# Feed-forward layers in three pieces of 8, 7 and 7 tile pairs, with weight slots of 1024 columns

## The chip, the cores and the metric

The kernel runs on one core of a Trainium2 chip, as one launch that holds the whole network. The metric is the device time of one execution in microseconds (us); three executions of the kernel before are given with their median. A profiled execution of the same kernel supplies the trace that is quoted here. In it PE is TensorE (matmuls), PEld its weight loads, DVE is VectorE, ACT ScalarE, POOL GpSimd, SP SyncE (it only issues DMAs here).

## The reference: what is computed

Two layers act on 256 latent tokens (stream 0) and 256 context tokens (stream 1), width 1024. Each layer is a half-step feed-forward, a token mixer (layer 0: neighbourhood attention beside a Hyena operator; layer 1: retention), and another half-step feed-forward. Every step is modulated: vectors of shift, scale and gate come from one large matrix applied to a conditioning vector.

```python
def modulate(x, gain, shift, scale):
    return rms_norm(x, gain) * (1 + scale) + shift

def swiglu(h, w_in, w_out):
    a, b = jnp.split(h @ w_in, 2, axis=-1)
    return (jax.nn.silu(a) * b) @ w_out
...
x_lat = x_lat + 0.5 * mod_l[:, 2] * swiglu(modulate(x_lat, norm_gain[i, 0], mod_l[:, 0], mod_l[:, 1]),
                                           ffn_a_in[i], ffn_a_out[i])
```

`w_in` is 1024 by 5632, `w_out` 2816 by 1024, so the hidden width 2816 is 22 tiles of 128 for `a` and 22 for `b`: 22 pairs. There are four such layers here. Three treat both streams; the last treats the latent stream alone, since nothing reads the context after it.

## The kernel before: tiling, staging and order

Activations are kept with features on partitions: a tile is 128 features by 512 columns, stream 0 in columns 0 to 255 and stream 1 in 256 to 511. Every product is done in three matmuls (L208, L209, L210), because weights and activations are each split into a high and a low part: high by high, low activation by high weight, high activation by low weight.

**Weights** form one long list, `worder`, in the order in which they are used. `w_dma` (L138) loads the next tile of the list into a slot of pool `wraw` on SP's queue. `w_split` makes the high part on ACT (`whi`, L89) and the low part on DVE (`wlo`, L153) into pool `whl`, and then issues one more load. `w_get(ahead)` first splits up to `ahead` tiles beyond the wanted one. Before, both pools have four slots of 11 x 128 = 1408 columns. An input tile (`ffi`) has 1024 columns, an output tile (`ffo`) has 1408. `w_paged` splits a tile into pages of 512 columns instead (`wphi`, `wplo`), from a general pool.

**A feed-forward layer** (`ffn`) goes in two halves of 11 pairs. For each pair two input tiles of 24 matmuls each run (`pi`), then `evac` makes silu(a) x b: silu on ACT, the product on DVE (`sg`, L580), the high part on ACT (`ghi`, L89) and the low part on DVE (`glo`, L181). After 11 pairs `out_gemm` runs the output: for each of 8 output tiles m the 11 x 3 matmuls of the half (`po`), then one DVE instruction for each stream adds gate times the sum to the residual `x` (L391). Both halves add to the same `x`.

**The modulation vectors** of later steps are made beside all this, on DVE: `mod_step` takes one tile of the modulation matrix and runs one or two reductions of 1024 columns (L237, `junk`): two where both streams need the vector, one where only the latent stream does (the last 32 of the 128 tiles). Two steps follow each pair's `evac`, and one step each output tile of `out_gemm`, except from m = 4 on where a norm follows. The steps work off one list of 128 tiles and stop when it is empty.

**The end of the last half** is special, because the next step's norm must be hidden. With `norm` given, every `x` is also squared on ACT and added up in `acc` on DVE (L269). The last `ntail` output tiles run stream 0 first, for all of them; then part of stream 1 of the first of them; then a matmul of ones (`ss`, L296) sums `acc` of stream 0; then the rest of stream 1. While that runs, ACT and DVE compute the inverse root (L283 to L287) and the first normed blocks (`nh` L308, `hhi` on ACT, `hlo` L313). `first_group` then begins the next step's matmuls (`fg`): two blocks of stream 0, then the matmul `ss` of stream 1, and so on. `ntail` is 3 where the output has 8 tiles of depth (the first mixer), and 2 where it has 11 (the feed-forward layers).

Nothing reorders the instructions: each engine runs its own in the order in which the Python code issues them, and waits in place.

Of the kernel before, what the change touches and what calls it, by code (L numbers as in the profile page):

```python
# [16 lines left out]
P = 128  # L17
D = 1024
KB = D // P
# [1 line left out]
TOK = 2 * L  # L21
DFF = 2816
NJ = DFF // P
NH = NJ // 2
EPS = 1e-6
MAGIC = 12582912.0
TWO_PI = float(np.nextafter(np.float32(2 * math.pi), np.float32(0)))
LOG_SET = "natural_log_exp_and_others"
WSLOT = NH * P


C_GAIN = 0
# [22 lines left out]
def body(ctx, tc, I, out):  # L55
    nc = tc.nc
    V, S, T, SY, G = nc.vector, nc.scalar, nc.tensor, nc.sync, nc.gpsimd

    wraw = ctx.enter_context(tc.tile_pool(name="wraw", bufs=4))
    whl = ctx.enter_context(tc.tile_pool(name="whl", bufs=4))  # L60
    modp = ctx.enter_context(tc.tile_pool(name="modp", bufs=2))
    one = ctx.enter_context(tc.tile_pool(name="one", bufs=1))
    pagep = ctx.enter_context(tc.tile_pool(name="pagep", bufs=1))
# [46 lines left out]
        worder.append((I[name][idx], n))  # L110

    def add_ffn(i):
        for h in range(2):
            for j in range(h * NH, (h + 1) * NH):
                add_w("ffi", (i, 2 * j), KB * P)
                add_w("ffi", (i, 2 * j + 1), KB * P)
            for m in range(KB):
                add_w("ffo", (i, h, m), NH * P)

    add_ffn(0)  # L120
    for b in range(24 + 8):
# [257 lines left out]
    def out_gemm(acts, nk, tiles_per_m, l, n, lat_only, norm, late_acts=None):  # L379
# [18 lines left out]
            for fn in late:  # L398
                fn()

        ntail = 3 if nk == KB else 2
        last_full = KB - ntail if (norm and not lat_only) else KB
        for m in range(last_full):
            if m == 0 and late_acts:
# [27 lines left out]
        if not norm:  # L432
            return
        ws = [w_get(3 - i) for i in range(ntail)]
        wfirst.extend(w_get(0) if i < 4 - ntail else w_paged() for i in range(3))
        pp = [ps(name="po") for _ in range(ntail)]
        for i in range(ntail):
            mm(pp[i], 0, L, [ws[i]], 0, L)
            run(evac(pp[i], 0, 0, last_full + i))
        cut = 5 if nk > KB else KB  # L440
        mm(pp[0], L, TOK, [ws[0]], L, TOK, 0, cut)
        norm.stream(0)
        mm(pp[0], L, TOK, [ws[0]], L, TOK, cut, nk)
# [22 lines left out]
    def first_group(norm, mid=None):  # L466

        w = list(wfirst)
        wfirst.clear()
        p = [ps(name="fg") for _ in range(4)]  # L470

        def mm(t, k, s):
            mm3k(p[t][:, s * L:(s + 1) * L], w[t], k, H[k], s * L, (s + 1) * L)

        for k in range(KB):
            for t in range(3):
                mm(t, k, 0)
            if k == 1:
                st = norm.steps(1)
                for kk in range(4, KB):  # L480
                    norm.blocks(0, (kk,))
                    next(st, None)
                norm.flush()
                norm.done(0)
                w.append(w_get(0))
                norm.blocks(1, range(KB))
                norm.flush()
                norm.done(1)
        for k in range(KB):
            mm(3, k, 0)  # L490
        w_split()
        for k in range(KB):
            for t in (0, 1):
                mm(t, k, 1)
        w_split()
        w_split()
        if mid:
            mid(p)
        for k in range(KB):
            for t in (2, 3):  # L500
                mm(t, k, 1)
        w_drop(w[2])
        return p

# [65 lines left out]

    def ffn(l, n, norm_in, norm_out, lat_only=False):
        w = L if lat_only else TOK
        for h in range(2):
            Gt = []

            def evac(pa, pb, shift=None):
                sg = page([P, w], name="sg")
# [13 lines left out]
            if h == 0:  # L591
# [14 lines left out]
                    p = first_group(norm_in, lambda p: evac(p[0], p[1]))  # L606
                    evac(p[2], p[3])
                j0 = len(Gt)
            for j in range(j0, NH):
                pa = in_tile(0, w)  # L610
                pb = in_tile(0, w)
                evac(pa, pb)
                if next(FILT["gen"], True):
                    mod_step(2)
            if h == 1:
                h_free()
            if h == 0:
                set_gate(l, n)
            pend_free.extend(Gt)
            out_gemm(Gt, NH, 1, l, n, lat_only, norm_out if h == 1 else None)  # L620
            free_acts()


# [828 lines left out]
def _layout(inp):  # L1452
# [49 lines left out]
    for l in range(2):  # L1502
        for nm in "ab":
            t_ = feat_tiles(g[f"ffn_{nm}_in"][l], 0)
            ffi.append(np.stack([t_[:NJ], t_[NJ:]], axis=1).reshape(2 * NJ, P, D))
            wo = g[f"ffn_{nm}_out"][l]
            ffo.append(np.stack([feat_tiles(wo[h * NH * P:(h + 1) * NH * P], 0) for h in range(2)]))
    z["ffi"] = np.stack(ffi)
    z["ffo"] = np.stack(ffo)

    def tok_tiles(w):
        C = w.shape[1]
# [64 lines left out]
```

## Time and profile before

| | |
|---|---|
| three runs | 1879.28, 1880.52, 1880.73 us; median 1880.52 us |
| profiled execution | 1878.3 us |
| its span, first to last instruction | 1876.5 us |
| mean granted TensorE clock in it | 0.997 |
| PE busy | 1857.1 us, 9974 matmuls |
| DVE busy | 1205.4 us |
| ACT busy | 701.5 us |
| POOL busy | 131.0 us |

The profiled execution took 1.8 us more than its span, and 2.2 us less than the median of the runs. A row of a timeline shows the start in us from the span's start, the duration, engine, line, operation, what it writes and reads, and how often it came in a row ("x2"); in brackets the idle time of the engine before it, and what ended it. A duration includes a tail that overlaps the next instruction, so the pace of a row of instructions is read from start to start. A row of a table of stretches shows the stretch, its length, the busy time of PE, PEld, DVE, ACT and POOL with the number of instructions, the granted clock, the DMA share and GB/s.

### The profile page before, as it was taken

The numbers are of one execution on the slowest core, as the hardware profiler recorded it, in microseconds if no ns is written. First come the engines' busy times: TensorE is split into PE (matmuls) and PEld (weight loads), VectorE is DVE, ScalarE is ACT, GpSimd is POOL, SyncE is SP. The second block draws the span as 40 slices with busy tenths as digits, with TensorE's granted clock in tenths as the row PEclk, the third lists the DMA queues.
The fourth block names the chain that finished last, engine by engine and source line by source line (L and its number), as shares of the span: only waits on it lengthen the run. The fifth ranks groups of instructions, "written<-read, shape, count | busy, mean of one in ns | idle before, by whom it ended". The sixth has DMA issues, their size and how long they took to land.

```text
span 1876.5 us, 25048 instructions
## 1 busy us (share of the span) xinstructions
PE 1857.1 (99%) x9974; PEld 1574.5 (84%) x9974; DVE 1205.4 (64%) x1858; ACT 701.5 (37%) x1085; POOL 131.0 (7%) x201
## 2 busy tenths in 40 slices
PE   8999999999999999999999999999999999999999
PEld 5788888898777898888888988888889888899999
DVE  5577677867687767866775655433456765567554
ACT  4332122335574342212233432122234454455342
POOL 2020000002003001100010001000000111000000
PEclk9999999999999999999999999999999999999999
DMA  9356445522323425644563356323323423355653
GB/s 361 127 176 218 144 169 206 197 79 80 101 70 100 145 69 185 217 160 158 195 231 112 108 189 220 101 90 108 106 85 97 140 90 101 104 183 187 190 186 130
DMA packets 77895, 277.45 MB, mean 148 GB/s; under 512 B 8657, under 2 KB 9681, under 8 KB 77650
## 3 DMA queue, kind: packets, MB, share of 16 engines
q1 hardware_dynamic: 58194, 206.64, 32.2%
q0 software_dynamic: 19584, 69.21, 11.7%
q8 instruction: 78, 1.28, 0.3%
q14 instruction: 39, 0.32, 0.1%
HBM read 274.77 MB, written 1.05 MB: 147 GB/s over the span
## 4 chain that ended last, share of the span: by engine, by line
PE 96%; DVE 2%; ACT 1%; issue 0%; DMA 0%; POOL 0%; DVEq 0%; ACTq 0%; POOLq 0%
PE pi L208 16%; PE pi L209 16%; PE pi L210 16%; PE po L210 9%; PE po L208 9%; PE po L209 9%; PE fg L208 2%; PE fg L210 2%; PE fg L209 2%; PE pv L1323 2%; PE pv L1324 2%; PE pv L1322 2%; PE pg L1324 1%; PE pg L1323 1%; PE pg L1322 1%
## 5 line engine op out<-in xcount | busy, mean ns | idle before, releaser
L208 PE MATMUL pi<-hhi,whi 128*128 128x512 f32 (+1 forms) x1488 | 544.2, 366 | 0.0
L209 PE MATMUL pi<-hlo,whi 128*128 128x512 f32 (+1 forms) x1488 | 543.9, 366 | 0.0
L210 PE MATMUL pi<-hhi,wlo 128*128 128x512 f32 (+1 forms) x1488 | 543.2, 365 | 0.0
L153 DVE TENSOR_TENSOR wlo<-raw,whi 128x1024 fp32r<-128x1024 f32 (+1 forms) x325 | 422.0, 1314 | 165.1 <-ACT whi L89 164.8
L89 ACT ACTIVATE whi<-raw 128x1024 fp32r<-128x1024 f32 (+1 forms) x329 | 364.4, 1116 | 418.8 <-issue 182.7
L208 PEld LDWEIGHTS pi<-hhi,whi 128*128 128x128 f32 x1488 | 279.3, 188 | 51.7 <-issue 1.5
L210 PEld LDWEIGHTS pi<-hhi,wlo 128*128 128x128 f32 x1488 | 279.3, 188 | 48.8
L209 PEld LDWEIGHTS pi<-hlo,whi 128*128 128x128 f32 x1488 | 279.4, 188 | 48.2
L237 DVE CUSTOM_DVE_ANT_0 junk<-wm,scb,cst 128x1024 bf16<-128x1024 f32 x224 | 287.3, 1283 | 14.1 <-DMA wm<-in_wmt_dram 9.0
L208 PE MATMUL po<-ghi,whi 128*128 128x512 f32 (+1 forms) x770 | 269.0, 349 | 0.0
L210 PE MATMUL po<-ghi,wlo 128*128 128x512 f32 (+1 forms) x770 | 268.4, 349 | 0.0
L209 PE MATMUL po<-glo,whi 128*128 128x512 f32 (+1 forms) x770 | 268.1, 348 | 0.0
L89 ACT ACTIVATE ghi<-sg 128x512 fp32r<-128x512 f32 (+1 forms) x88 | 50.9, 579 | 344.9 <-DVE sg L580 341.7
L209 PEld LDWEIGHTS po<-glo,whi 128*128 128x128 f32 x770 | 144.9, 188 | 20.4
L210 PEld LDWEIGHTS po<-ghi,wlo 128*128 128x128 f32 x770 | 144.9, 188 | 20.3
L208 PEld LDWEIGHTS po<-ghi,whi 128*128 128x128 f32 x770 | 144.8, 188 | 20.3
L391 DVE SCALAR_TENSOR_TENSOR x<-po,gate,x 128x256 f32<-128x256 f32 x136 | 61.4, 481 | 152.6 <-PE po L210 152.4
L580 DVE TENSOR_TENSOR sg<-sg,pi 128x512 f32<-128x512 f32 (+1 forms) x79 | 49.2, 622 | 138.1 <-PE pi L210 138.1
L222 POOL DMA_DIRECT2D wm<-in_wmt_dram x128 | 67.7, 529 | 785.5 <-DVE mod L237 766.2
L181 DVE TENSOR_TENSOR glo<-sg,ghi 128x512 fp32r<-128x512 f32 (+1 forms) x88 | 55.1, 626 | 56.9 <-ACT ghi L89 56.9
L89 ACT ACTIVATE sq<-x 128x256 f32<-128x256 f32 (+1 forms) x71 | 30.2, 439 | 132.5 <-DVE x L391 132.4
L208 PE MATMUL fg<-hhi,whi 128*128 128x256 f32 (+1 forms) x200 | 60.0, 300 | 0.0
(333 smaller groups left out, 2232.1 us busy)
## 6 DMA issues: line engine op xcount, KB each, us to landing
raw<-in_ffi_dram SPq DMA_DIRECT2D x176, 512.0 KB, 4.2
wm<-in_wmt_dram POOLq DMA_DIRECT2D x128, 512.0 KB, 3.8
raw<-in_ffo_dram SPq DMA_DIRECT2D x64, 704.0 KB, 5.4
raw<-in_rt_dram SPq DMA_DIRECT2D x64, 512.0 KB, 3.6
raw<-in_ev_dram SPq DMA_DIRECT2D x32, 512.0 KB, 3.6
wm<-in_wm_dram SPq DMA_DIRECT2D x32, 256.0 KB, 5.4
x<-in_xt_dram SPq DMA_DIRECT2D x8, 256.0 KB, 4.9
bias<-in_rpb_dram SPq DMA_DIRECT2D x8, 256.0 KB, 4.1
```

Source lines behind the costliest of these rows:

```text
L89: S.activation(out=out, in_=in_, func=func, **k)
L153: V.tensor_tensor(out=lo[:, :n], in0=t[:, :n], in1=f(hi[:, :n]), op=ALU.subtract)
L181: V.tensor_tensor(out=lo, in0=src, in1=f(hi), op=ALU.subtract)
L208: T.matmul(o, lhsT=w[0][:, c0:c1], rhs=x[0][:, x0:x1], start=start, stop=False)
L209: T.matmul(o, lhsT=w[0][:, c0:c1], rhs=x[1][:, x0:x1], start=False, stop=False)
L210: T.matmul(o, lhsT=w[1][:, c0:c1], rhs=x[0][:, x0:x1], start=False, stop=stop)
L222: G.dma_start(out=t, in_=I["wmt"][n])
L237: V.tensor_tensor_reduce(out=junk, in0=t, in1=scb[:, s, :], scale=1.0, scalar=bcol, op0=ALU.mult, op1=ALU.add, accum_out=MOD[l][:, idx, b, ...
L391: V.scalar_tensor_tensor(out=xs(s, m), in0=p[:, c0:c0 + L], scalar=gate[:, m, s:s + 1], in1=xs(s, m), op0=ALU.mult, op1=ALU.add)
L1322: T.matmul(po[tb], lhsT=H[k][0][:, hs_], rhs=w[0][:, ws_], start=k == 0, stop=False)
L1323: T.matmul(po[tb], lhsT=H[k][0][:, hs_], rhs=w[1][:, ws_], start=False, stop=False)
L1324: T.matmul(po[tb], lhsT=H[k][1][:, hs_], rhs=w[0][:, ws_], start=False, stop=k == KB - 1)
```

## The change

Each feed-forward layer goes in three pieces of 8, 7 and 7 pairs. All three add into `x`. The output weights are three arrays (`ffo0`, `ffo1`, `ffo2`) with 1024, 896 and 896 columns a tile; the arithmetic is the same, only grouped differently. The slot of both weight pools shrinks to 1024 columns, `wraw` gets six slots and `whl` five.

The conditions follow: `ntail` is 3 where the depth is at most 8, so now for the feed-forward layers too; of the first three weight tiles of the next step two come through `w_get` and one through `w_paged`, in the first mixer too (before, one and two there); and `cut`, the depth of stream 1 that the first tail tile runs ahead of the matmul `ss`, is at most the depth itself, 7, so all of that tile's stream 1 stands ahead of it (before, 5 of 11).

```diff
-NH = NJ // 2
+PIECES = ((0, 8), (8, 15), (15, 22))
-WSLOT = NH * P
+WSLOT = KB * P
...
-    wraw = ctx.enter_context(tc.tile_pool(name="wraw", bufs=4))
-    whl = ctx.enter_context(tc.tile_pool(name="whl", bufs=4))
+    wraw = ctx.enter_context(tc.tile_pool(name="wraw", bufs=6))
+    whl = ctx.enter_context(tc.tile_pool(name="whl", bufs=5))
...
     def add_ffn(i):
-        for h in range(2):
-            for j in range(h * NH, (h + 1) * NH):
+        for h, (j0, j1) in enumerate(PIECES):
+            for j in range(j0, j1):
                 add_w("ffi", (i, 2 * j), KB * P)
                 add_w("ffi", (i, 2 * j + 1), KB * P)
             for m in range(KB):
-                add_w("ffo", (i, h, m), NH * P)
+                add_w(f"ffo{h}", (i, m), (j1 - j0) * P)
...
-        ntail = 3 if nk == KB else 2
+        ntail = 3 if nk <= KB else 2
...
-        wfirst.extend(w_get(0) if i < 4 - ntail else w_paged() for i in range(3))
+        wfirst.extend(w_get(0) if i < 5 - ntail else w_paged() for i in range(3))
...
-        cut = 5 if nk > KB else KB
+        cut = min(5 if nk > KB else KB, nk)
...
+        w_drop(w[1])
         w_drop(w[2])
...
-        for h in range(2):
+        for h, (jf, jl) in enumerate(PIECES):
             Gt = []
+            last = h == len(PIECES) - 1
...
-            for j in range(j0, NH):
+            for j in range(jf + j0, jl):
...
-            if h == 1:
+            if last:
                 h_free()
...
-            out_gemm(Gt, NH, 1, l, n, lat_only, norm_out if h == 1 else None)
+            out_gemm(Gt, jl - jf, 1, l, n, lat_only, norm_out if last else None)
```

Where the instructions stand shows on DVE, at the end of the first feed-forward layer. First place: output tile m = 1 of its last piece, from the low part of the weights that is split ahead of it to the one after it. Before:

```order
L153 TENSOR_TENSOR wlo<-raw,whi 128x1408
L391 SCALAR_TENSOR_TENSOR x_94<-po,gate,x_94 128x256
L391 SCALAR_TENSOR_TENSOR x_102<-po,gate,x_102 128x256
L269 TENSOR_TENSOR acc<-acc,sq 128x256 x2
L237 ISA junk,mod_85<-wm,scb,cst 128x1024
L237 ISA mod_85 128x1
```

and now:

```order
L153 TENSOR_TENSOR wlo<-raw,whi 128x896
L391 SCALAR_TENSOR_TENSOR x_94<-po,gate,x_94 128x256
L391 SCALAR_TENSOR_TENSOR x_102<-po,gate,x_102 128x256
L269 TENSOR_TENSOR acc<-acc,sq 128x256 x2
L237 ISA junk,mod_85<-wm,scb,cst 128x1024
L237 ISA mod_85 128x1
```

The last two rows come twice for each such tile, in both. What a tile asks of DVE is the same but for the width of the weights, 896 columns and not 1408, while PE's share of the tile goes from 33 matmuls to 21.

Second place: the tail of the same layer, on DVE, from the last tile that runs both streams together to the last sum of stream 0. Before:

```order
L391 SCALAR_TENSOR_TENSOR x_106<-po,gate,x_106 128x256
L269 TENSOR_TENSOR acc<-acc,sq 128x256 x2
L153 TENSOR_TENSOR wlo<-raw,whi 128x1024
L181 TENSOR_TENSOR wplo<-raw,wphi 128x512 x2
L391 SCALAR_TENSOR_TENSOR x_100<-po,gate,x_100 128x256
L269 TENSOR_TENSOR acc<-acc,sq 128x256
L391 SCALAR_TENSOR_TENSOR x_100<-po,gate,x_100 128x256
L269 TENSOR_TENSOR acc<-acc,sq 128x256
```

and now:

```order
L391 SCALAR_TENSOR_TENSOR x_106<-po,gate,x_106 128x256
L269 TENSOR_TENSOR acc<-acc,sq 128x256 x2
L153 TENSOR_TENSOR wlo<-raw,whi 128x1024 x2
L181 TENSOR_TENSOR wplo<-raw,wphi 128x512 x2
L391 SCALAR_TENSOR_TENSOR x_98<-po,gate,x_98 128x256
L269 TENSOR_TENSOR acc<-acc,sq 128x256
L391 SCALAR_TENSOR_TENSOR x_100<-po,gate,x_100 128x256
L269 TENSOR_TENSOR acc<-acc,sq 128x256
L391 SCALAR_TENSOR_TENSOR x_100<-po,gate,x_100 128x256
L269 TENSOR_TENSOR acc<-acc,sq 128x256
```

One more low part of weights and one more residual tile of stream 0 stand ahead of the last sum.

Third place: DVE right behind the matmul `ss` of stream 0 in the same layer, up to the first normed block. Before:

```order
L287 SCALAR_TENSOR_TENSOR rr<-rs_m,rr 128x256
L308 SCALAR_TENSOR_TENSOR nh<-x_94,gs_88,rr 128x256
L391 SCALAR_TENSOR_TENSOR x_108<-po,gate,x_108 128x256
L308 SCALAR_TENSOR_TENSOR nh<-x_94,gs_88,rr 128x256
L313 SCALAR_TENSOR_TENSOR hlo<-nh,mod_85,hhi 128x256
```

and now:

```order
L287 SCALAR_TENSOR_TENSOR rr<-rs_m,rr 128x256
L391 SCALAR_TENSOR_TENSOR x_106<-po,gate,x_106 128x256
L269 TENSOR_TENSOR acc<-acc,sq 128x256
L308 SCALAR_TENSOR_TENSOR nh<-x_94,gs_88,rr 128x256
L391 SCALAR_TENSOR_TENSOR x_108<-po,gate,x_108 128x256
L308 SCALAR_TENSOR_TENSOR nh<-x_94,gs_88,rr 128x256
L313 SCALAR_TENSOR_TENSOR hlo<-nh,mod_85,hhi 128x256
```

A residual tile of stream 1 and its sum have moved ahead of the first normed block.

More of the change, by code (lines that the diff above doesn't have):

```diff
@@ L1506, in _layout @@
             wo = g[f"ffn_{nm}_out"][l]
-            ffo.append(np.stack([feat_tiles(wo[h * NH * P:(h + 1) * NH * P], 0) for h in range(2)]))
+            ffo.append([feat_tiles(wo[j0 * P:j1 * P], 0) for j0, j1 in PIECES])
     z["ffi"] = np.stack(ffi)
-    z["ffo"] = np.stack(ffo)
+    for h in range(len(PIECES)):
+        z[f"ffo{h}"] = np.stack([o[h] for o in ffo])
     def tok_tiles(w):
```

## The prediction

> **What bounds the kernel now.** I read the page's first part, then the chain that ended last, then the table of stretches, then PE's waits.
>
> ```profile
> PE 1857.1 (99%) x9974; PEld 1574.5 (84%) x9974; DVE 1205.4 (64%) x1858; ACT 701.5 (37%) x1085; POOL 131.0 (7%) x201
> PE 96%; DVE 2%; ACT 1%; issue 0%; DMA 0%; POOL 0%; DVEq 0%; ACTq 0%; POOLq 0%
> ```
>
> PE is busy for 1857.1 of 1876.5 us. All that any change of order or buffers could win is the rest, 19.4 us. The stretches show where that rest lies and how fast a PE that never waits goes:
>
> ```profile
> 0.00:50.00 50.00, 41.91 (x205) 27.32 (x206) 28.40 (x76) 21.38 (x41) 9.61 (x33) 0.97 1.01 362
> ...
> 400.00:500.00 100.00, 98.36 (x568) 84.62 (x567) 67.90 (x113) 53.37 (x96) 10.71 (x8) 1.00 0.25 81
> 500.00:600.00 100.00, 97.24 (x552) 76.17 (x551) 79.49 (x165) 57.39 (x157) 10.83 (x11) 0.98 0.28 93
> 600.00:700.00 100.00, 96.46 (x616) 87.12 (x616) 74.06 (x127) 43.36 (x73) 10.09 (x11) 0.98 0.31 103
> ...
> 1200.00:1300.00 100.00, 100.00 (x433) 80.94 (x432) 34.21 (x39) 25.08 (x31) 0.00 (x0) 1.00 0.28 89
> ...
> 1700.00:1800.00 100.00, 100.00 (x853) 100.00 (x852) 61.92 (x78) 48.54 (x70) 0.00 (x0) 1.00 0.61 190
> 1800.00:1877.00 77.00, 73.26 (x623) 73.06 (x622) 38.42 (x45) 28.23 (x36) 0.00 (x0) 0.99 0.47 151
> ```
>
> The row at 1200 lies inside a feed-forward layer: 433 matmuls of 512 columns touch these 100 us, so 432 steps of 0.2315 us, none lost. The row at 1700, with 256 columns, gives 0.117 us. In the first mixer (400 to 700) PE idles 1.6, 2.8 and 3.5 us, 7.9 in all; 8.1 lie in the first 50 us and 3.7 in the last 77. The feed-forward layers between have no idle time to win. The question is what the change makes PE wait for, and the answer must come from DVE, which each piece loads anew.
>
> **The change part by part. PE's own work** does not move. The matmuls of 512 and 256 columns are the same in number but for 6 halves that become 3 wholes in each of three tails (6 x 0.117 against 3 x 0.2315: nothing). A new output tile costs PE no gap, as the full rows above contain such switches. Eight more output tiles for each layer are eight more sets of residual updates on DVE, 0.79 us each (357.00 to 357.79, below), beside PE's 4.9 us for a tile.
>
> **Piece boundaries.** An output tile needs the last pair's `glo` at its last depth: now 22 matmuls (depth 8) or 19 (depth 7) after its start, not 31.
>
> ```profile
> 130.55 0.39 PE L208 MATMUL pi<-hhi,whi 128*128 128x512 f32 x1
> 132.38 0.69 DVE L181 TENSOR_TENSOR glo<-sg,ghi 128x512 fp32r<-128x512 f32 x1 [0.83 <-ACT ghi L89]
> ...
> 1841.80 0.28 PE L208 MATMUL po<-ghi,whi 128*128 128x256 f32 x1
> 1842.98 0.42 DVE L181 TENSOR_TENSOR glo<-sg,ghi 128x256 fp32r<-128x256 f32 x1 [0.48 <-ACT ghi L89]
> ```
>
> The first two rows are the end of pair 7 of the first layer, where piece 0 will end. DVE is late there, and still `glo` lands at 133.07, 2.5 us after PE goes on; PE would ask for it 22 x 0.2315 = 5.1 us after. The last two are the one-stream layer, the tightest: `glo` lands 1.6 us after the start, and 19 x 0.117 = 2.2 us are allowed. Cost 0; with DVE 3 us later than that it would be 0.5 us at a two-stream boundary and 2.4 at a one-stream one.
>
> **Buffers.** The loads and splits keep their order; deeper pools only let them run sooner. In the whole trace PE's waits name a weight split twice:
>
> ```profile
> PE fg L878 <- DVE wlo L170: 0.3, 1, 0.3
> PE po L210 <- DVE wlo L153: 0.2, 1, 0.2
> ```
>
> So a gain of at most 0.5 us here; I take 0 and leave what lies beyond to a rival.
>
> **The tails** are where I find the cost. From now on the feed-forward tails have the form of the first mixer's tail: `ntail` 3. So its rows price them.
>
> ```profile
> 646.41 0.28 PE L208 MATMUL po<-chi,whi 128*128 128x256 f32 x1
> ...
> 657.82 0.59 PE L296 MATMUL ss<-acc,cst 128*128 128x256 f32 x2
> ...
> 666.52 0.70 PE L296 MATMUL ss<-acc,cst 128*128 128x256 f32 x2 [0.28 <-DVE acc L269]
> ...
> 646.62 0.88 DVE L391 SCALAR_TENSOR_TENSOR x<-po,gate,x 128x256 f32<-128x256 f32 x2
> ...
> 656.13 0.43 DVE L269 TENSOR_TENSOR acc<-acc,sq 128x256 f32<-128x256 f32 x1 [0.48 <-ACT sq L89]
> ...
> 666.04 0.42 DVE L269 TENSOR_TENSOR acc<-acc,sq 128x256 f32<-128x256 f32 x1
> ```
>
> From the first `ss` (657.82) to the second (666.52) are 8.70 us, and the second waited for DVE's `acc`, which ended at 666.46: a chain on DVE sets this. Now the feed-forward tail before:
>
> ```profile
> 1026.63 0.64 PE L296 MATMUL ss<-acc,cst 128*128 128x256 f32 x2
> ...
> 1035.29 0.59 PE L296 MATMUL ss<-acc,cst 128*128 128x256 f32 x2
> ```
>
> 8.66 us, with no wait on the second: here PE sets it, with 51 + 18 = 69 half-width matmuls between the two. Now 42 + 18 = 60 stand there (two tails of 7 x 3, not 18 + 33), so PE needs 8.66 - 9 x 0.117 = 7.61, while DVE gets the mixer's list and needs 8.70. PE waits 1.1 us for each tail; the nine matmuls have gone ahead of `ss`, where they hide nothing that was open. **Three tails: 3.3 us.**
>
> Ahead of `ss`, the mixer's DVE chain takes 656.56 - 646.62 = 9.94 us from the residual of the last whole tile (m = 4) to the end of `acc`: one `wlo`, four `wplo` and three residual tiles with their sums. The changed list is one `wlo` of 1024 more for two `wplo` fewer:
>
> ```profile
> 396.15 1.22 DVE L153 TENSOR_TENSOR wlo<-raw,whi 128x1024 fp32r<-128x1024 f32 x1 [0.52 <-ACT whi L89]
> 397.30 1.29 DVE L181 TENSOR_TENSOR wplo<-raw,wphi 128x512 fp32r<-128x512 f32 x2
> 398.50 0.48 DVE L391 SCALAR_TENSOR_TENSOR x<-po,gate,x 128x256 f32<-128x256 f32 x1
> ```
>
> 1.15 against 1.20 us from start to start: the same. PE covered it in the mixer with 96 half matmuls, 657.82 - 646.41 = 11.41 us, and `ss` came 1.26 after `acc` was done. Now it has 7 x 3 x 4 = 84, which is 84 x 11.41 / 96 = 9.98 us. DVE needs 646.62 - 646.41 + 9.94 + 0.06 (from `acc` to `ss`, 666.46 to 666.52) = 10.21. So `ss` waits 0.2 us where DVE reaches m = 4 on time.
>
> In the first layer it does not. Its last piece begins with DVE behind, since the modulation steps of the last pair (four reductions) follow `glo`:
>
> ```profile
> 348.01 0.39 PE L208 MATMUL po<-ghi,whi 128*128 128x512 f32 x1
> ...
> 355.46 1.62 DVE L153 TENSOR_TENSOR wlo<-raw,whi 128x1408 fp32r<-128x1408 f32 x1
> 357.00 0.87 DVE L391 SCALAR_TENSOR_TENSOR x<-po,gate,x 128x256 f32<-128x256 f32 x2
> 357.79 1.28 DVE L237 CUSTOM_DVE_ANT_0 junk<-wm,scb,cst 128x1024 bf16<-128x1024 f32 x1
> ...
> 360.32 1.62 DVE L153 TENSOR_TENSOR wlo<-raw,whi 128x1408 fp32r<-128x1408 f32 x1
> ...
> 363.42 0.88 DVE L391 SCALAR_TENSOR_TENSOR x<-po,gate,x 128x256 f32<-128x256 f32 x2 [1.48 <-PE po L210]
> 364.39 0.82 DVE L269 TENSOR_TENSOR acc<-acc,sq 128x256 f32<-128x256 f32 x2
> 365.12 1.28 DVE L237 CUSTOM_DVE_ANT_0 junk<-wm,scb,cst 128x1024 bf16<-128x1024 f32 x1
> ```
>
> Counted from PE's first output matmul (348.01), the reductions end at 7.45. A `wlo` of 1408 costs 1.54 from start to start, one of 1024 1.15; on that line 896 cost 1.02 (an estimate). So m = 0's residual starts at 8.47, and m = 0 takes 0.79 + 2.53 + 1.02, which brings m = 1 at 12.81. A tile with sums takes 0.97 + 0.73 + 2.53 + 1.02 = 5.25 us of DVE; PE's 21 matmuls take 4.86. Before, 5.8 stood against 7.6, and the lag was gone by m = 1 (the idle 1.48 above). Now it grows: m = 2 at 18.06, m = 3 at 23.31, m = 4 at 28.56. PE has finished m = 4 at 105 x 0.2315 = 24.3 and comes to `ss` at 24.3 + 9.98 = 34.3; DVE is ready at 28.56 + 9.94 + 0.06 = 38.56. **`ss` waits 4.3 us.** Queued behind it on PE are the rest of stream 1 and the next step's first group; nothing else could run. The bounds: 0.2, if DVE is on time there as in the other layers, and 6.9, if a `wlo` of 896 cost what one of 1408 does (five times 0.52 more). I take the middle, since both its rows, 1024 and 1408, were measured.
>
> The other two tails have less: in layer 0's second feed-forward one reduction per step is left, in the third none (the list of 128 is empty: 8 + 8 + 14 + 8 + 14 + 4 = 56 steps in the first layer, 4 in the mixer, 60 in the second, 8 left).
>
> ```profile
> 976.12 1.62 DVE L153 TENSOR_TENSOR wlo<-raw,whi 128x1408 fp32r<-128x1408 f32 x1
> ...
> 979.92 1.27 DVE L237 CUSTOM_DVE_ANT_0 junk<-wm,scb,cst 128x1024 bf16<-128x1024 f32 x1
> ```
>
> A tile costs DVE 5.25 - 1.27 = 4.0 us there, under 4.86, so it catches up: 0.2 each. Both pieces ahead of the last also stay level: without sums a tile takes 4.34 (896 columns) or 4.47 (1024) against 4.86 and 5.56.
>
> **PE's clock** adds a little. After the longest wait of the trace it was halved for a while:
>
> ```profile
> PE ptc L1074 <- DVE prc L1054: 2.5, 1, 2.5
> 500.00:512.00 12.00, 9.52 (x54) 7.78 (x53) 10.56 (x23) 6.40 (x17) 0.00 (x0) 0.86 0.40 132
> ```
>
> 0.86 over 12 us is half speed for 3.4 us, 1.7 us of matmuls. A wait of 4.3 us should do the same, behind the first `ss`; 1.1 us of that is the wait of the DVE chain anyway, so 0.6 are left (bounds 0 and 1.7). The Trainium skill ("TensorE: Matmul & The Clock Gate", Part 1: The HAM clock gate) has the clock drop after at least one idle window of about 3.4 us, windows that run free of the program. The trace differs: a wait of 2.5 us was enough. By that rule 4.3 us would mostly not hold a whole window, the term would be 0, and the sum 8.0.
>
> **Sum:** 3.3 + 4.3 + 0.2 + 0.2 + 0.6 = 8.6 us on the profiled 1878.3 (span and 1.8 around it): 1886.9. The median of the runs is 2.2 above that execution, so 1889 for the time.
>
> **The rivals.** *DVE is on time in the first layer too*: a reduction list shorter than counted, or DVE ahead by then. Against it stands the idle of only 1.48 us at m = 1 above. Then 3.3 + 3 x 0.2 = 3.9, time 1884.4. *Nothing is lost*: the DVE chain gives way, because the last sums come earlier than in the mixer's list; time 1880.5, but the list is the same row by row. *Faster*: a fifth pair of slots ends waits of ACT for PE, and ACT and DVE then come sooner in the first mixer.
>
> ```profile
> ACT whi L89 <- PE po L209: 160.4, 31, 6.6
> ```
>
> ACT waits long for slots, but in the output stages, where PE does not wait. Where PE waits (7.9 us, in the mixer) DVE, ACT and POOL run a chain that no weight slot holds. It decides only if a split that waits for its slot stands ahead of that chain on ACT; half of the 7.9 won gives 1876.5. *Worse*: the lag also delays the weights of the last output tile. Its `wlo` ends as m = 4's residual starts, 28.56, and PE asks for it at 24.3 + 42 x 0.119 = 29.3; with 2 us more lag PE stops there, and each of the three tails halves the clock: 8.6 + 2 + 2 x 0.6 = 11.8, time 1892.3.
>
> **How the numbers follow.** Forecast 0.52, on time 0.14, nothing 0.14, faster 0.09, worse 0.11. The forecast's own range is 1886 to 1891. The whole range, 1880 to 1893, takes in the bounds and leaves out most of the faster case and part of the worse. What differs by less than 0.2% (3.8 us) cannot be told from no change here. The on-time case stands at that bound and is split: slower 0.52 + 0.11 + 0.09 = 0.72, within 0.2% 0.14 + 0.05 = 0.19, faster 0.09.
>
> **What would show it.** PE's waits would list `ss` on DVE `acc` with some 8 us in total, up to 4 or 5 us in one piece behind the first layer's last output tiles, and about 1 us at each second `ss`; DVE would show no idle time from that layer's last pair to the first `ss`. The order of the waits in the first mixer should stay. Wrong would be: no long wait at the first `ss`, waits of PE at a piece's first output tile, or PE idle in the mixer clearly under 7.9 us.

## The result and the profile after

| | before | after |
|---|---|---|
| runs, us | 1879.28, 1879.94, 1880.52, 1880.73 | 1890.61, 1890.66, 1891.17, 1891.35 |
| median, us | 1880.23 | 1890.91 |
| profiled execution, us | 1878.3 | 1891.17 |
| its span, us | 1876.5 | 1889.4 |
| mean granted clock | 0.997 | 0.995 |

The changed kernel is slower: the ratio of the runs is 1.0061, with an interval of 1.0049 to 1.0073, and the two medians of the table lie 10.7 us apart. The forecast was 1889. In the changed kernel's trace the lines behind `first_group` have moved by one or two (the product on DVE is L582, not L580; `ptc` L1076, not L1074).

The page of the changed kernel, the rows that answer to the first two of the prediction (busy time, then the chain of work that ended last):

```profile
PE 1864.8 (99%) x9965; PEld 1579.4 (84%) x9965; DVE 1225.2 (65%) x1945; ACT 705.4 (37%) x1116; POOL 130.6 (7%) x201
PE 76%; issue 13%; DVE 5%; DMA 4%; ACT 1%; POOL 1%; POOLq 0%; DVEq 0%; ACTq 0%
```

The chain was 96% PE before and is 76% PE now. PE is no less busy; the chain leaves PE because at one place PE waits for DVE, and from there it runs back along DVE's work, the loads of modulation tiles (DMA) and time that the profile puts down to no wait (issue). How far back it runs says nothing of the cost: in a second profile of the changed kernel, with nearly the same wait, the chain is 92% PE. PE's waits in the changed kernel name the place (total, times, longest, in us):

```profile
PE po L208 <- DVE x L391: 3.5, 1, 3.5
PE ptc L1076 <- DVE prc L1056: 2.5, 1, 2.5
...
PE ss L296 <- DVE acc L269: 1.4, 4, 0.4
...
PE fg L209 <- DVE hlo L313: 0.6, 3, 0.2
...
PE po L210 <- DVE wlo L153: 0.2, 1, 0.2
```

The first row is new. The 2.5 us of `ptc`, in the first mixer, stood in the trace before too. Here is the chain around the new wait (start, length, what):

```profile
384.02 1.29 DVE junk L237
...
402.44 1.00 DVE wlo L153
403.44 0.41 DVE x L391
403.87 0.44 ACT sq L89 x2
...
406.81 1.22 DVE wlo L153
408.03 1.20 DVE wplo L181 x2
409.23 0.41 DVE x L391
409.63 0.04 issue
409.68 0.58 PE po L208
```

From 384.02 to 409.68 the named pieces are DVE's, or ACT's for DVE: reductions (`junk`), low parts of weights, residuals. The pieces of 1.2 us that the chain calls issue there (not shown) lie under DVE's second reduction of each step. And PE at that place:

```profile
405.95 0.28 PE L210 MATMUL po<-ghi,wlo 128*128 128x256 f32 x1
409.68 0.58 PE L208 MATMUL po<-ghi,whi 128*128 128x256 f32 x1 [3.45 <-DVE x L391]
410.06 0.42 PE L209 MATMUL po<-glo,whi 128*128 128x256 f32 x1
...
412.83 0.32 PE L210 MATMUL po<-ghi,wlo 128*128 128x256 f32 x1
412.99 0.28 PE L208 MATMUL po<-ghi,whi 128*128 128x256 f32 x1
...
413.71 0.60 PE L296 MATMUL ss<-acc,cst 128*128 128x256 f32 x2
...
422.23 0.70 PE L296 MATMUL ss<-acc,cst 128*128 128x256 f32 x2 [0.38 <-DVE acc L269]
```

PE has finished stream 0 of the three tail tiles at 406.1. Its next matmul writes stream 1 of the first of them, the other half of a tile whose stream 0 DVE has not read yet, and it starts right behind that read. After the wait the halves take 0.21 us from start to start, and 0.12 again from 412.99 on. The stretches of the changed kernel show this as the granted clock, 0.93 over 25 us; that is half speed for 3.5 us (0.07 x 25 / 0.5):

```profile
400.00:425.00 25.00, 20.97 (x157) 20.26 (x156) 19.99 (x42) 11.38 (x25) 0.00 (x0) 0.93 0.34 118
500.00:600.00 100.00, 97.51 (x574) 76.38 (x571) 79.17 (x177) 60.53 (x170) 4.72 (x6) 1.00 0.26 89
600.00:700.00 100.00, 96.35 (x609) 86.66 (x608) 77.58 (x132) 44.17 (x75) 16.23 (x15) 0.97 0.30 106
1200.00:1300.00 100.00, 100.00 (x434) 81.04 (x433) 37.44 (x48) 25.82 (x31) 0.00 (x0) 1.00 0.31 95
```

The idle time of PE from 500 to 700 is 6.1 us, before 6.3: the first mixer's waits have stayed.

To see where the 12.9 us between the two profiled spans lie, the next table cuts each kernel at matmuls of PE's timeline: the first `pi`, the second `ss` of each tail, the first `pi` of the last layer. The columns to the right of "after" are experiments below.

| stretch, us | before | after | steps taken away | 8, 6, 8 | 8, 4, 10 | before, pools moved | before, weight pools exchanged |
|---|---|---|---|---|---|---|---|
| start | 55.8 | 58.7 | 59.3 | 58.3 | 56.7 | 59.2 | 59.0 |
| feed-forward 1 | 356.1 | 363.5 | 358.6 | 358.2 | 358.3 | 358.2 | 356.1 |
| mixer 1 | 254.6 | 254.7 | 256.3 | 254.3 | 256.3 | 256.6 | 253.3 |
| feed-forward 2 | 368.8 | 369.0 | 369.1 | 369.3 | 369.4 | 368.3 | 368.8 |
| feed-forward 3 | 369.0 | 369.5 | 369.6 | 369.2 | 368.9 | 368.5 | 369.0 |
| mixer 2 | 299.5 | 300.6 | 300.6 | 300.5 | 300.7 | 300.6 | 299.6 |
| feed-forward 4 and end | 172.7 | 173.3 | 173.3 | 174.6 | 173.9 | 173.4 | 172.7 |
| span | 1876.5 | 1889.4 | 1886.8 | 1884.4 | 1884.1 | 1884.6 | 1878.5 |

Of the 12.9 us, 7.4 lie in the first feed-forward layer and 3.0 ahead of it, where PE's instructions are the same. Layers 2 and 3 lost only 0.2 and 0.5, though each has its new waits. The second mixer and the last layer lost 1.0 and 0.6 without any.

The row of the first mixer needs care. Its length goes by how often the clock is halved there. These are the stretches of 10 us around the second half-speed stretch of the mixer, first in the kernel before, then with 8, 4 and 10 pairs:

```profile
612.00:622.00 10.00, 9.16 (x53) 8.41 (x52) 5.09 (x8) 3.01 (x5) 1.48 (x2) 0.83 0.18 52
```

```profile
615.00:625.00 10.00, 9.16 (x46) 8.70 (x47) 4.74 (x7) 2.10 (x4) 1.78 (x2) 0.66 0.17 52
```

A clock of 0.83 over 10 us is half speed for 3.4 us, and 0.66 is 6.8 us: 1.7 us more of lost time, which is the whole difference in that row, 256.3 against 254.6. In the other profiles too the halved time in this mixer is 3.4, 6.8 or 10.2 us in all, so a difference of 1.7 us in that row is one more or one fewer such stretch, and no measure of PE's pace.

### The profile page after: what moved, and what is told of

It reads as the page before. It is cut to its first block, busy times and chain, and to the rows that moved or that the text cites. A ratio compares the mean times of both kernels' runs of the same rounds, so it can differ in the third digit from the quotient of the medians.

```text
span 1889.4 us, 25275 instructions
## 1 busy us (share of the span) xinstructions
PE 1864.8 (99%) x9965; PEld 1579.4 (84%) x9965; DVE 1225.2 (65%) x1945; ACT 705.4 (37%) x1116; POOL 130.6 (7%) x201
## 4 chain that ended last, share of the span: by engine, by line
PE 76%; issue 13%; DVE 5%; DMA 4%; ACT 1%; POOL 1%; POOLq 0%; DVEq 0%; ACTq 0%
PE pi L208 12%; PE pi L209 12%; PE pi L210 12%; PE po L208 7%; PE po L210 7%; PE po L209 7%; DMA wm<-in_wmt_dram 4%; PE fg L208 2%; PE fg L210 2%; PE fg L209 2%; PE pv L1324 2%; PE pv L1325 2%; PE pv L1326 2%; PE pg L1325 1%; PE pg L1326 1%
## 5 line engine op out<-in xcount | busy, mean ns | idle before, releaser
L153 DVE TENSOR_TENSOR wlo<-raw,whi 128x1024 fp32r<-128x1024 f32 (+1 forms) x358 | 424.3, 1212 | 55.8 <-ACT whi L89 54.6
L582 DVE TENSOR_TENSOR sg<-sg,pi 128x512 f32<-128x512 f32 (+1 forms) x79 | 49.2, 623 | 253.6 <-PE pi L210 253.6
L391 DVE SCALAR_TENSOR_TENSOR x<-po,gate,x 128x256 f32<-128x256 f32 x192 | 86.3, 479 | 103.4 <-PE po L210 102.9
L89 ACT ACTIVATE sg<-pi 128x512 f32<-128x512 f32 (+1 forms) x79 | 43.1, 546 | 150.4 <-PE pi L210 150.1
L208 PE MATMUL fg<-hhi,whi 128*128 128x256 f32 (+1 forms) x216 | 64.5, 299 | 0.0
```

The source lines that it names most:

```text
L89: S.activation(out=out, in_=in_, func=func, **k)
L153: V.tensor_tensor(out=lo[:, :n], in0=t[:, :n], in1=f(hi[:, :n]), op=ALU.subtract)
L208: T.matmul(o, lhsT=w[0][:, c0:c1], rhs=x[0][:, x0:x1], start=start, stop=False)
L391: V.scalar_tensor_tensor(out=xs(s, m), in0=p[:, c0:c0 + L], scalar=gate[:, m, s:s + 1], in1=xs(s, m), op0=ALU.mult, op1=ALU.add)
L582: V.tensor_tensor(out=sg, in0=sg, in1=pb[:, :w], op=ALU.mult)
```

## The experiments

**The two kernels once more**, to see which of these differences come back.

> The kernel before, unchanged, profiled once more, to see which differences between the two first profiles belong to an execution and not to the change. In the first pair the changed kernel reached its first whole input tile at 58.72 us, not 55.76, and its half-clock stretch at the start was 6.8 us and not 3.4. Theory (the start depends on where the program meets the clock's windows): the first input tile comes anywhere from 55 to 60 us here, and the steps of 512-column matmuls stay within 0.2% of 0.2315 us, stage by stage not the same as in the first profile. Rival (the start is fixed for a program, and the change made it 3 us slower): 55.8 us again, within 0.3.

> The changed kernel, profiled once more. Theory (the 3.0 us at the start are of the execution): first input tile anywhere from 55 to 60 us; the wait of PE for DVE in the first layer's last piece is there again, 3 to 4 us in one piece, and the two sums of stream 0 and 1 are 8.5 to 8.7 us apart in all three tails. Rival (deeper pools bring two more weight loads into the start and cost 3 us): 58.7 us again, within 0.3.

Measured: 1879.09 and 1890.58 us. In both, the stretches of feed-forward layers 2 to 4 and of the second mixer came back within 0.02 us, and the new wait of the changed kernel too:

```profile
PE po L208 <- DVE x L391: 3.0, 1, 3.0
PE ss L296 <- DVE acc L269: 1.3, 4, 0.4
```

Its first `pi` came at 58.3 us, that of the kernel before at 56.4. So the 0.5 to 1 us in stretches without a wait belong to the program and are no accident of an execution. For the start this decides little: each kernel came back 0.4 to 0.6 us from its first profile, more than the rival's 0.3 and far less than the 5 us that the theory allows.

**The steps beside the last output tiles taken away.** In the feed-forward layers no modulation step stands beside the output tiles of the last piece; the list is worked off later, and the output is the same.

```diff
-            if m < 4 or not norm:
+            if not norm or (m < 4 and nk == KB):
                 mod_step()
```

> The changed kernel, but the last piece of a feed-forward layer runs no modulation step beside its first four output tiles (they go later, to the second and third layer). Theory (DVE falls behind in the first layer's last piece, because a tile with two reductions takes 5.25 us there and PE's 4.86): DVE is level at output tile 1, the wait of PE of 3.5 us and the halved clock behind it are gone; 5 us less than the changed kernel, about 1886 (1885 to 1887). The two other layers keep their 1.1 us at the second sum. Rival (the tail's form alone or the number of pieces costs the time): within 1 us of 1891.

Measured: 1885.98 us (1883.64 to 1888.53), ratio 1.0038 [1.0025, 1.0051]. DVE catches up and idles ahead of m = 4; first a row of its timeline, then the stretch around the tail, then the page's chain of waits:

```profile
399.43 0.88 DVE L391 SCALAR_TENSOR_TENSOR x<-po,gate,x 128x256 f32<-128x256 f32 x2 [1.58 <-PE po L210]
```

```profile
395.00:420.00 25.00, 24.35 (x180) 22.83 (x180) 18.28 (x40) 12.50 (x26) 0.00 (x0) 1.00 0.31 106
```

```profile
PE 94%; DVE 4%; ACT 1%; issue 1%; DMA 0%; POOL 0%; DVEq 0%; POOLq 0%; ACTq 0%
```

The 3.5 us wait is gone from its list of waits, the clock is 1.00 there, PE idles 0.65 us in these 25 and not 4.03, the chain is 94% PE, and layer 1 is 4.9 us shorter (table; 4.94 up to the first `ss`). Of the rest the four waits of `ss` stay, 1.4 us together, as in the changed kernel. So the lag of DVE, fed by the reductions beside output tiles that now take PE less time, costs 4.9 us with the clock that follows it.

**Another order of the pieces.** With 7, 7 and 8 pairs the last output has depth 8: PE has 24 matmuls for each tile, as in the mixer's tail.

```diff
-PIECES = ((0, 8), (8, 15), (15, 22))
+PIECES = ((0, 7), (7, 14), (14, 22))
```

> The changed kernel with pieces of 7, 7 and 8 pairs, so that the last one is the longest. Theory (the last piece's PE time per output tile and per tail tile is what matters): a tile gives DVE 5.56 us and asks 5.38, the first layer's wait goes; 66 half matmuls stand between the two sums, not 60, so each tail waits 0.4 us, not 1.1. 5 + 3 x 0.7 = 7 us less, about 1884 (1883 to 1885.5). Rival (three pieces cost by their 8 more residual updates a layer and their boundaries): no change, 1890 to 1892.

Measured: 1890.75 us (1884.64 to 1891.54), ratio 1.0053 [1.0034, 1.0072]. Both kinds of tail waits went as the theory says, and still nothing was won. PE's waits show a new one of the same size:

```profile
PE po L210 <- DVE wlo L153: 3.2, 2, 3.1
...
PE ss L296 <- DVE acc L269: 0.2, 1, 0.2
```

It stands at the end of the first piece. DVE there:

```profile
136.24 1.28 DVE L237 CUSTOM_DVE_ANT_0 junk<-wm,scb,cst 128x1024 bf16<-128x1024 f32 x1 [0.57 <-DMA wm<-in_wmt_dram]
...
137.57 1.28 DVE L237 CUSTOM_DVE_ANT_0 junk<-wm,scb,cst 128x1024 bf16<-128x1024 f32 x1
...
138.90 0.17 DVE L328 TENSOR_SCALAR gate<-mod 128x16 f32<-128x16 f32 x1
138.98 1.09 DVE L153 TENSOR_TENSOR wlo<-raw,whi 128x896 fp32r<-128x896 f32 x1
```

The layer's gate needs eight modulation tiles. The first four pairs of this layer carry no steps, so eight pairs make eight tiles and seven make six. So the two missing steps run in one go ahead of the first output weights, and PE stops for the low part of these (140.12). DVE also idled there for the loads of their tiles, 0.57 us in the first row and 1.74 us ahead of the step before it. The expectation had looked at the tails alone. A first piece of 8 pairs has this for free.

**8, 6 and 8 pairs** keep the first piece and give the last one the depth 8.

```diff
-PIECES = ((0, 8), (8, 15), (15, 22))
+PIECES = ((0, 8), (8, 14), (14, 22))
```

> The changed kernel with pieces of 8, 6 and 8 pairs. With 7, 7 and 8 the first layer's late wait had gone, but PE waited 3.1 us for a weight split at the end of its first piece. Theory (that piece had run 6 of the 8 modulation steps that its gate needs, so two more were forced in front of the weight split): with 8 pairs in it all 8 are done, both waits are gone, about 1885.9 (1885 to 1887), 5 us less than with 7, 7 and 8. Rival (a short piece makes the split late wherever it stands): the wait returns at the end of the 6-pair piece, 1889 or more.

Measured: 1886.75 us (1881.88 to 1889.89), ratio 1.0037 [1.0024, 1.0049]. PE's waits:

```profile
PE ss L296 <- DVE acc L269: 0.7, 4, 0.2
...
PE po L210 <- DVE wlo L153: 0.2, 1, 0.2
```

Both new waits are gone or at 0.2 us, with all modulation steps in place. This is the theory's second confirmation: 24 matmuls for a tile (5.56 us) cover DVE's 5.38 (5.25, and 0.13 for a `wlo` of 1024 columns), 21 (4.86) do not cover 5.25, and layer 1 is 5.3 us shorter than in the changed kernel (table). Layers 2 and 3 got about 0.3 us longer and about as much shorter, although their waits at the sums went down as well, so what these waits cost in time is read from the trace and not shown by this run. And 7.5 us over the kernel before are left, which no wait explains. Part of them is the clock: the ten executions stand in the order of their mean granted clock, 1881.9 to 1882.2 us at 0.999, 1884.6 to 1886.1 at 0.997 and 1887.4 to 1889.9 at 0.995, while the kernel before had 0.996 or 0.997 in all its executions beside them. A clock lower by 0.004 is 7.5 us of 1885 (an estimate), about the whole spread. That the median fell on the 1885.9 expected is therefore in part luck. At 0.997 it is still about 4 us or more above the kernel before.

**The buffers.** Four slots in each pool, as before, with the three pieces.

```diff
-    wraw = ctx.enter_context(tc.tile_pool(name="wraw", bufs=6))
-    whl = ctx.enter_context(tc.tile_pool(name="whl", bufs=5))
+    wraw = ctx.enter_context(tc.tile_pool(name="wraw", bufs=4))
+    whl = ctx.enter_context(tc.tile_pool(name="whl", bufs=4))
...
-        wfirst.extend(w_get(0) if i < 5 - ntail else w_paged() for i in range(3))
+        wfirst.extend(w_get(0) if i < 4 - ntail else w_paged() for i in range(3))
```

> The changed kernel with four slots in both weight pools, as before, of 1024 columns. Theory (the deeper pools neither win nor cost: the waits are DVE's order of work): waits of PE as in the changed kernel, time within 1 us of it, 1890 to 1892. For the start, 2.6 us later in the changed kernel than before in two profiles each: if the two further early loads do that, the first whole input tile comes at 55.5 to 56.5 us here; if not, at 58 to 59.5. Rival for the mixer (deeper slots free ACT): its segment gets longer by 1 us or more here.

Measured: 1892.8 us (1892.09 to 1894.98), ratio 1.0072 [1.0056, 1.0088], above the 1890 to 1892 expected. The waits are those of the changed kernel (2.8 us for the long one), the first mixer is 0.4 us longer and not 1, and the first input tile came at 56.3 us, as it should if the early loads cost time at the start. What differs is the pace without a wait: 432 matmuls in the stretch from 1200 to 1300, not 434.

```profile
1200.00:1300.00 100.00, 100.00 (x432) 80.81 (x432) 37.12 (x47) 24.86 (x30) 0.00 (x0) 1.00 0.31 94
```

With `wraw` alone back at four slots:

> The changed kernel with four slots for raw weights and five for the split ones. In five profiles with six raw slots the first whole input tile came at 58.3 to 59.3 us, in four with four slots at 55.8 to 56.7. Theory (six slots let two more loads into the start): 55.5 to 57 here. Rival (the five split slots do it, or the meeting with the clock's windows, by chance): 58 to 59.5.

Measured: 1891.39 us in one execution, span 1889.6; its stretches are within 0.15 us of the changed kernel's, but for the start. The fifth and sixth slot of `wraw` bring nothing, and the theory on the start fell: the first input tile came at 59.1 us with four slots. The five split slots do not decide it either: the changed kernel with its pools moved has five and came at 55.8, and the kernel before with its weight pools exchanged has four and came at 59.0 (both below). What the fifth slot of `whl` does to the pace stays open, since taking it away also moved every buffer behind it.

**Pieces that let DVE breathe.** 8, 4 and 10 pairs with the slots of before, `ntail` 2 in the last piece, and no modulation step beside the output tiles of the piece of 4:

```diff
-NH = NJ // 2
+PIECES = ((0, 8), (8, 12), (12, 22))
-WSLOT = NH * P
+WSLOT = 11 * P
...
-            if m < 4 or not norm:
+            if nk != 4 and (m < 4 or not norm):
                 mod_step()
```

> Three pieces again, but of 8, 4 and 10 pairs, with the slots (four of 1408 columns) and the tail (two tiles) of the kernel before; the 4-pair piece runs no modulation steps. So each layer still has 8 more residual updates and one more boundary, but its last piece gives DVE 6.9 us a tile. Theory (not the number of pieces costs, but the short last piece): waits of PE at most 0.2 us a layer and 0.5 in the one-stream layer, 1 to 2 us above before. Rival (each further piece costs by itself): 4 us or more above before.

Measured: 1885.94 us (1883.05 to 1888.57), ratio 1.0038 [1.0028, 1.0048]. That is 6.7 us slower, not 1 or 2, and by the number the rival is met. The trace speaks against it: the one new wait is 0.6 us in the last layer (from start to start), and the loss does not go with the pieces. Layer 1 has +2.2, layer 2 +0.6, layer 3 -0.1 and the last layer +1.2, with the same pieces in each, and the second mixer +1.1, whose work is unchanged. The +1.7 of the first mixer is the clock, as shown above, and the start has +0.9. So there is a second cause in the stretches where PE never waits: its pace.

**The pools moved, nothing else.** The kernel before, with its two weight pools opened behind the pool of pages. All buffers change their place in SBUF; no instruction changes.

```diff
-    wraw = ctx.enter_context(tc.tile_pool(name="wraw", bufs=4))
-    whl = ctx.enter_context(tc.tile_pool(name="whl", bufs=4))
...
+    wraw = ctx.enter_context(tc.tile_pool(name="wraw", bufs=4))
+    whl = ctx.enter_context(tc.tile_pool(name="whl", bufs=4))
```

(the added lines stand behind the pool `pagep`).

> The kernel before with its buffers at other places in SBUF and not one instruction changed: the two weight pools are opened behind the pages and not ahead of them. In two profiles of one kernel PE's time from stage to stage agrees within 0.02 us outside the clock's half-speed stretches, while kernels that differ only in buffers and pieces have stages 0.3 to 1.5 us apart with no wait to show for it: the mean step of a 512-column matmul is 230.6 in one and 231.9 ns in another, and each place within a tile has its own step. Theory (the step depends on where the operands lie): the steps change here, some stages by 0.3 us or more, either way, waits as before; in all up to 4 us. Rival (it depends on the instructions and their waits): every stage outside the half-speed stretches within 0.05 us of before.

> The changed kernel with the same exchange of places and no instruction changed. The wait of 3 us for DVE in the first layer and the 1.1 us at each second sum must stay, whatever the theory. Theory (place sets the step): stages without a wait, the second mixer and the one-stream layer above all, differ from the changed kernel by 0.3 us or more. Rival (instructions set it): within 0.05 us.

Measured: 1885.33 us (1884.0 to 1886.38) for the kernel before, ratio 1.0031 [1.0019, 1.0044]; 1891.13 (1887.82 to 1892.16) for the changed one, ratio 1.0061 [1.0046, 1.0076]. So 5.9 us come to the kernel before from places alone, more than the 4 expected, and its waits are as they were. The same stretch of its first layer, first as it is and then with the pools moved:

```profile
160.00:260.00 100.00, 100.00 (x435) 81.13 (x434) 69.29 (x100) 20.98 (x22) 7.92 (x15) 1.00 0.49 166
```

```profile
160.00:260.00 100.00, 100.00 (x432) 80.93 (x431) 70.25 (x101) 22.37 (x23) 7.94 (x15) 1.00 0.45 155
```

PE is busy for all 100 us at full clock in both, and does three matmuls fewer. The table has the sign both ways: layer 1 +2.1, layers 2 and 3 -0.5 each, second mixer +1.0, last layer +0.7. These, some 2.7 us together, are pace. The rest of the 8.1 us between the two profiles is 3.5 us in the start and 1.9 in the first mixer, of which 1.7 are the clock; so less than half of the 5.9 is shown to be pace. In sign these are the shifts that the changed kernel shows beside its waits, and in size they are within 0.7 us of them (worked out below). In the changed kernel the same exchange kept the waits (3.4 us for the long one) and moved layers 2, 3 and 4 by +0.4, -0.8 and +0.7, layer 1 not. The second mixer, named first in the expectation, moved by 0.02 us only, so there the theory missed.

**Only the weight pools exchanged** (`whl` opened ahead of `wraw`), the pages where they were:

> The kernel before with the two weight pools opened in the other order: raw and split weights trade places, every page and constant stays where it was, and no instruction changes. With all places exchanged the second mixer took 1.04 us more and the feed-forward layers between 0.5 us less and 2.1 us more, without a wait. Theory (the place of the split weights takes part in the step): the feed-forward stages change again, by 0.3 us or more in at least two of the four; the second mixer may stay, since in the changed kernel it did not answer to a move of the weights alone (0.02 us). Rival (only the pages' places count): every stage outside the half-speed stretches within 0.05 us of before, time 1878 to 1881.

Measured: 1879.69 us (1878.14 to 1880.41), ratio 0.9998 [0.9989, 1.0008]. Every stretch but the start and the first mixer is that of the kernel before within 0.05 us. So this move of the two weight pools does nothing to the pace. What is left is the place of the pools that moved in the run before and not in this one: the pages, where the activations lie, the constants and the modulation tiles. That it is the pages is likely and not shown, since no run moved them alone. What property of the place decides was not found either: with `wraw` at four slots the buffers behind it lie 8192 bytes elsewhere (two slots of 1024 columns of 4 bytes), and the changed kernel's pace stayed.

No version tried beats the kernel before.

## Why the prediction was right

**The direction and the bound**: slower, by PE waiting for DVE, at the ends of the pieces. Shown: the wait and the work on DVE ahead of it, and the two runs that took the wait away in different ways (fewer steps on DVE, more matmuls on PE).

**The lag of DVE** was predicted tile by tile from PE's first output matmul. In the changed kernel that matmul starts at 374.22; DVE's timeline:

```profile
382.68 0.87 DVE L391 SCALAR_TENSOR_TENSOR x<-po,gate,x 128x256 f32<-128x256 f32 x2
384.02 1.29 DVE L237 CUSTOM_DVE_ANT_0 junk<-wm,scb,cst 128x1024 bf16<-128x1024 f32 x1 [0.47 <-DMA wm<-in_wmt_dram]
...
398.13 0.87 DVE L391 SCALAR_TENSOR_TENSOR x<-po,gate,x 128x256 f32<-128x256 f32 x2
...
402.36 1.09 DVE L153 TENSOR_TENSOR wlo<-raw,whi 128x896 fp32r<-128x896 f32 x1
403.36 0.87 DVE L391 SCALAR_TENSOR_TENSOR x<-po,gate,x 128x256 f32<-128x256 f32 x2
...
409.15 0.47 DVE L391 SCALAR_TENSOR_TENSOR x<-po,gate,x 128x256 f32<-128x256 f32 x1
...
412.71 0.42 DVE L269 TENSOR_TENSOR acc<-acc,sq 128x256 f32<-128x256 f32 x1 [0.48 <-ACT sq L89]
```

| after PE's first `po`, us | predicted | measured |
|---|---|---|
| residual of m = 0 | 8.47 | 8.46 |
| one tile to the next (m = 3 to 4) | 5.25 | 5.23 |
| residual of m = 4 | 28.56 | 29.14 |
| last `acc` of stream 0 done | 38.50 | 38.91 |

The 0.5 us too few at m = 4 are the wait for a modulation tile at 384.02. A `wlo` of 896 columns takes 1.00 us from start to start (1.02 estimated).

**Where PE waits** was wrong, though not its price. The prediction let PE run through stream 1 of the first tail tile and stop at `ss`. By its own signs it should have been seen in some 8 us of `ss` on `acc`; the list has 1.4 us there, and the first `ss` has no long wait at all, which the prediction had named as a sign of being wrong. PE stopped ahead of that stream, because both streams share the tile that DVE has yet to read. That is read from the releaser in the trace; no run gave the streams separate tiles. That moves 2.5 us of matmuls from before the wait to behind it, and with the full clock they would still have fitted in ahead of the end of `acc`: 409.68 + 2.5 = 412.2 against 413.13. At half clock they ended at 413.7, so `ss` came 0.5 us late. Without any lag `ss` would have come 2.5 us after the end of stream 0, at 406.07 + 2.5 = 408.6; it came at 413.71, 5.1 us later. Predicted: 4.3 + 0.6 = 4.9. The price held because DVE's lag was right and `ss` came within 0.6 us of the same last `acc`.

**The clock.** The prediction took half speed after the wait and 0.6 us for it; 0.5 was paid. That the two are so close is luck: the 0.6 was meant for matmuls behind the first `ss`, and the 0.5 came ahead of it, as what the halved stream 1 overran the end of `acc`. The wait of 2.5 us that it reasoned from is also not the longest of the trace; one of 4.5 us for a load stands at the very start (`pf`). It also weighed the Trainium skill's rule ("TensorE: Matmul & The Clock Gate", Part 1: The HAM clock gate): windows of about 3.4 us that run free of the program, at least one of them idle. The half-speed stretch (some 3.5 us by the mean of 0.93) agrees with the length of the window, and a wait of 3.45 us was enough. The runs fit the free running as well: the `ptc` wait of 2.5 us in the first mixer was followed by half speed in one execution of the kernel before and not in another (the stretches of the first and second profile of the same kernel):

```profile
500.00:520.00 20.00, 17.52 (x101) 13.63 (x99) 15.73 (x39) 11.75 (x38) 0.00 (x0) 0.91 0.25 80
```

```profile
500.00:520.00 20.00, 17.51 (x110) 13.40 (x110) 16.99 (x43) 12.70 (x40) 0.00 (x0) 1.00 0.24 80
```

Against the rule as stated stands still that 2.5 us is less than a window.

**The three tails**, 1.1 us each, 3.3 in all. Between the two `ss` now lie 8.52, 8.59 and 8.60 us (8.70 predicted) with 60 matmuls; by the pace of before they would be 8.65 less 9 x 0.117, or 7.60. That is 0.9, 1.0 and 1.0: 2.9 for 3.3. Only a good half of it stands at the second `ss`. In each tail some 0.45 us come before, where the first group's second product waits for `hlo` (the row `fg` in the list of waits, which counts less because the tail of a matmul's duration hides the first part of a wait). The first `ss` of layers 2 and 3 cost 0.2 and 0.3 (0.2 each predicted): up to it, PE's gaps beyond the pace add up to 0.60 and 0.58 us, against 0.39 and 0.29 before.

**Piece boundaries and buffers**, 0 each: the list of waits after has only the 0.2 us of `wlo` there, as before, and with four slots in `wraw` every stretch but the start stayed. That the first boundary is free only from 8 pairs on, because of the gate, was not in the prediction; 7, 7 and 8 showed it.

**The sum** of these steps, as measured, is 5.1 + 2.9 + 0.5 = 8.5 us, against 8.6 predicted. Only the first of its terms was checked by taking it away (4.9 us). The medians differ by 10.7. The term that the prediction sized wrongly is PE's own work, "does not move" at 0.2315 us a matmul. In the changed kernel the step depends on the stage: layer 1 lost 7.4, of which 5.1 and 0.9 are the steps above, so 1.4 by pace; layers 2 and 3 won back about 1.0 and 0.8 of the 1.2 and 1.3 that their waits cost; the second mixer and the last layer lost 1.0 and 0.6. Together 1.2 us. That such shifts come from places alone is shown by the moved pools; that exactly these come from it is likely, by their signs and sizes, and not shown. About 1 us remains between 8.5 + 1.2 and 10.7. It would lie in the start and the clock of the first mixer, which differ by up to 3.6 and 3.2 us between the profiles; how much of that belongs to the change stays open.

**The rivals.** "DVE on time" and "nothing lost" fall by the 3.5 us wait; "faster" by the mixer's unchanged waits and the runs with fewer slots. "Worse" would have shown PE stopped at the last tile's `wlo`; the trace has no such wait.

## What to carry to other kernels

Where one engine hides another's work tile by tile, write both lists per tile before changing the tile: here 21 matmuls of 4.86 us stood over 5.25 us of DVE, a lag that grows with every tile and is paid at the first matmul that needs DVE's last word. Cutting work into more pieces keeps the main engine's sum and multiplies what the others do for each piece, so move the side work (here the modulation steps) or deepen the last piece together with the cut. And before a change of some tenths of a per cent is put down to its order of work, move the buffers of the old kernel alone and see what that does.

## What the runs showed of the hardware that was not expected

Places in SBUF change the pace of a PE that never waits. With identical instructions, 100 us held 435 matmuls of 512 columns or 432, at a granted clock of 1.00. The whole kernel took 5.9 us (0.31%) more; 2.7 us of the difference between the profiles lie in stretches without a wait and at full clock. For given places the pace returns within 0.02 us a stage from execution to execution.

The first 60 us differ by 3 us between kernels without any instruction being different, and by 0.4 to 0.6 us between two profiles of one kernel. In the stretch from 12 to 18 us PE is busy throughout; these are the kernel before and, in the second fence, the same with its weight pools exchanged:

```profile
12.00:18.00 6.00, 6.00 (x31) 4.91 (x34) 2.51 (x6) 3.00 (x5) 0.00 (x0) 1.00 1.05 388
```

```profile
12.00:18.00 6.00, 6.00 (x16) 4.59 (x16) 1.27 (x4) 2.98 (x5) 0.00 (x0) 1.00 1.05 389
```

Half as many matmuls in the same busy time, though the granted clock reads 1.00 in both. The changed kernel had 17 and, with its pools moved, 31. That it is the clock at its start is likely by the factor of two; no run here settled what decides it, and the places of the buffers are not ruled out.
